# One program order over the twelve scan units of an RWKV-7 layer, the pieces of an inverse loaded through GpSimd's queue, and the backward direction's products first

## The chip, the cores and the metric

The kernel runs on one core of a Trainium2 chip. The metric is device time in microseconds (us) of one execution; lower is better. The profiled execution is one such run, taken apart by the hardware profiler. Engine names as in the profile: PE (TensorE matmul), PEld (its weight loads), DVE (VectorE), ACT (ScalarE), POOL (GpSimd), SP (SyncE, which here only issues DMAs; SPq is its queue).

## The reference

A two-layer trunk over 512 latent tokens and 256 context tokens of width 1024, all in float32. Each layer is a half-SwiGLU, a token mixer, and a half-SwiGLU. The mixer of the second layer is a bidirectional RWKV-7, and only its recurrence is touched here:

```
S_t = S_{t-1} (diag(w_t) - kk_t^T (a_t kk_t)) + v_t^T k_t ,   y_t = S_t r_t
```

There are 16 heads with a 64 by 64 state each. The forward and the backward direction each run over the context tokens first and then, from that state, over the latent tokens; the two outputs are added.

## The kernel before, in words

The recurrence is computed in chunks of 64 tokens. Within a chunk the steps are tied together by a triangular matrix N (64 by 64 for each head, chunk and direction), and the chunk's solution needs the inverse of (1 - N). The work is cut into 12 **units**, `todo` (line 1596): four groups `qd` of four heads, and for each of them g = 0 (context), 1 and 2 (the two halves of the latents). A unit has 256 tokens of each direction; d = 0 is forward, d = 1 backward. What is done for a unit, in this order:

- `prep_a` (L1239): ten loads on SP, from `hw` at L1246 to L at L1260, then decays, then the products KR and BK (DVE, L1294 and L1297), then **A**: for each direction d and head pair e, 16 matmuls (L1320), which DVE masks out of PSUM into N and, for latents, Ar (L1327, four evictions). These use two PSUM banks for each step. Then N of the backward direction is transposed on DVE (NT, L1332), and the 16 by 16 diagonal blocks of both directions are scattered to DRAM, 16 DMAs on SP (L1335).
- `prep_m` (L1340): POOL loads the blocks from DRAM (M, L1347), inverts them all at once, one block to a partition, in 28 dependent operations (L1353 and L1354), and stores them (`me`, L1357).
- `prep_d` (L1361): 16 DMAs on SP lay the inverted blocks into a tile **X** (L1366), each 16 partitions by 8 runs of 64 bytes. Two X tiles alternate.
- `prep_v`, `prep_t`, `prep_b`: loads of v (VU, four DMAs on SP, L1376), transposes of BK (bkt), and the products kT and W, copied to KW on ACT.
- `prep_c` (L1410): doubles the inverse from 16 to 32 to 64. Step 1 transposes X's blocks on DVE (L1416), step 2 is T (PE, L1428), step 3 is R (L1435), and so on to Y; four steps YK (L1477) apply Y; five steps follow with P (L1491).
- `scan` (L1506): the state G over four chunks, and y.

A `readout` of a group's result follows every third unit, through banks and queues shared with the rest.

The main loop at the end of `rwkv_scan` has one iteration for each unit i. An iteration runs the scan of unit i, `prep_b` and `prep_c` of unit i + 1, the last five steps of `prep_a` (the A steps) and `prep_t`, `prep_m` of unit i + 2, and the first fifteen steps of `prep_a` of unit i + 3. At its end come `prep_v` and `prep_d` of unit i + 2. `laid` interleaves these: each stream is given a count of steps and a stretch (from, to) of the iteration, its steps are spread evenly over the stretch, and all are emitted in order of these positions. `tc.manual_schedule` around an iteration makes PE, DVE, ACT and SP issue that iteration's instructions in the order of emission. POOL is left to the scheduler, and so is where instructions of one such region fall among those of another on the same engine. Every engine executes its own instructions in order.

So one dependency goes round from iteration to iteration: X of a unit must have landed for DVE's transposes and PE's T in `prep_c`; A evictions stand behind these on DVE and A matmuls on PE; from the last A come NT, the scatter, POOL's inversion, and X of the next unit.

Of the kernel before, what the change touches and what calls it, by code (L numbers as in the profile page):

```python
# [73 lines left out]
def trunk(ctx, tc, io, phases=None, dump=None):  # L74
# [1109 lines left out]
    def rwkv_scan(l):  # L1184
# [11 lines left out]
        def Q(name):  # L1196

            if "B2" not in late:
                name = {"N": "Ar", "NT": "L"}.get(name, name)
            name = {"bvl": "N", "gl": "N", "q": "KW"}.get(name, name)  # L1200
            ring = RINGS2.get(name) if "B2" in late else None
            return (late["B2"] if ring else B1).tile([128, 1024], F32, tag=name, name=name, bufs=ring or RINGS1[name])
# [36 lines left out]
        def prep_a(qd, g):  # L1239
# [46 lines left out]
            for d in range(2):  # L1286
# [21 lines left out]
                dve.tensor_copy(g2[:, :, 3], Ev[:, :, chunk(d, 3), end])  # L1308
                dve.tensor_copy(gs[:, 2 * d:2 * d + 2], Eiv[:, :, chunk(d, 0), beg])
                yield  # L1310
            for d in range(2):

                N[d] = Q("N").rearrange("p (s n) -> p s n", n=64)
                if lat:
                    Ar[d] = Q("Ar").rearrange("p (s n) -> p s n", n=64)
                for e in range(2):
                    ps_ = [bank("A", "a") for _ in range(2)]
                    for c in range(4):
                        for hp in range(2):
                            pe.matmul(ps_[hp][:, 128 * c:128 * c + cols], BK[d][half(hp), 4 * e + c].rearrange("p s n -> p (s n)"),  # L1320
                                      KR[d][half(hp), 4 * e + c][:, :1 + lat], start=True, stop=True)
                    for hp in range(2):
                        pv = ps_[hp].rearrange("p (c s n) -> p c s n", s=2, n=64)
                        s0 = slot(hp, e, 0)
                        for s, dst in ((0, N[d]), (1, Ar[d])):
                            if dst is not None:
                                dve.tensor_tensor(dst[:, s0:s0 + 4], pv[:, :, s],  # L1327
                                                  masks[d][:, 64 * s:64 * s + 64].unsqueeze(1).to_broadcast([128, 4, 64]), ALU.mult)
                    yield

            NT_ = Q("NT").rearrange("p (s n) -> p s n", n=64)
            dve.transpose(NT_.rearrange("p s n -> p (s n)"), N[1].rearrange("p s n -> p (s n)"))  # L1332
            md = dram.tile([128, 16, 16], F32, tag="md", name="md", bufs=2)
            for d, hp, b, l0, r0 in lanes:
                nc.sync.dma_start(out=md[l0:l0 + 8].rearrange("l s t -> s l t"),  # L1335
                                  in_=(N[0] if d == 0 else NT_)[r0:r0 + 16, 8 * hp:8 * hp + 8, 16 * b:16 * b + 16])
            ready[qd, g] = KR, BK, N, Ar, gt, md
            yield

# [21 lines left out]
        def prep_d(qd, g):  # L1361
            me = inverse[qd, g]
            X = inverse[qd, g] = diagonal[(3 * qd + g) % 2]
            for d, hp, b, l0, r0 in lanes:
                o = 16 * (b % 2)
                nc.sync.dma_start(out=X[r0:r0 + 16, d, d, :, o:o + 16], in_=me[l0:l0 + 8].rearrange("l s t -> s l t"))  # L1366
            yield

        bkts, vus = {}, {}
# [40 lines left out]
        def prep_c(qd, g):  # L1410
# [60 lines left out]
            for d in range(2):  # L1471
                for e in range(2):
                    p = bank("YK")
                    pv = p.rearrange("p (c x n) -> p c x n", c=4, x=2)
                    for c in range(4):
                        for hp in range(2):
                            pe.matmul(p[half(hp), 128 * c:128 * c + 128], Y[half(hp), d, 4 * e + c], KW[d][half(hp), e, c].rearrange("p x n -> p (x n)"), start=True, stop=True)  # L1477
                    act.activation(KW[d][:, e, :, 0], pv[:, :, 0], AF.Copy)
                    for hp in range(2):
                        if hp:  # L1480
                            dve.tensor_copy(VU[half(hp), d, :, hp, e], pv[half(hp), :, 1])
                        else:
                            act.activation(VU[half(hp), d, :, hp, e], pv[half(hp), :, 1], AF.Copy)
                    yield
            for d in range(2):
                for e in range(2):
# [19 lines left out]
        def scan(qd, g, KR, Ar, BKT, VU, gt):  # L1506
            lat = g > 0
            if g == 1:
                state["y"] = late["B2"].tile([128, 2, TL], F32, tag="y", name="ybuf", bufs=2)
            yb = state.get("y")  # L1510
            G = state["G"] if lat else None
            at = lambda d, e: slice(64 * (2 * d + e), 64 * (2 * d + e) + 64)
            if g < 2:

                dve.tensor_tensor(gt[:, :, 3], gt[:, :, 3], decays[qd, g + 1], ALU.mult)
            Gs = []
            for i in range(4):
                cs = (i, 3 - i)
                Gs.append(G)
                if g < 2 or i < 3:  # L1520
                    p = bank("G", "s")
                    for n, (d, e) in enumerate(DE):
                        for hp in range(2):
                            pe.matmul(p[half(hp), at(d, e)], BKT[d][:, e, cs[d], half(hp)], VU[:, d, cs[d], hp, e], start=n == 0, stop=True, skip_group_check=n > 0)
                    if G is not None:
                        for n, (d, e) in enumerate(DE):
                            for hp in range(2):
                                pe.matmul(p[half(hp), at(d, e)], KR[d][half(hp), 4 * e + cs[d], 0], G[half(hp), 2 * d + e], start=False, stop=True, skip_group_check=True)
                    G = late["B2"].tile([128, 4, 64], F32, tag="G", name="G", bufs=NG)
                    dve.tensor_tensor(G, p[:, :256].rearrange("p (s n) -> p s n", n=64), gt[:, :, i].unsqueeze(2).to_broadcast([128, 4, 64]), ALU.mult)  # L1530
                    yield
            state["G"] = G
            for i in (1, 3) if lat else ():

                p = bank("y", "s")
                pv = p.rearrange("p (q d e n) -> p q d e n", q=2, d=2, e=2)
                two = [(q, d, e, hp) for q in range(2) for d, e in DE for hp in range(2)]
                where = lambda q, d: (i - 1 + q, q) if d == 0 else (4 - i - 1 + 1 - q, 1 - q)
                for n, (q, d, e, hp) in enumerate(two):
                    c, o = where(q, d)  # L1540
                    pe.matmul(pv[half(hp), o, d, e], VU[:, d, c, hp, e], Ar[d][:, slot(hp, e, c)], start=n < 2, stop=True, skip_group_check=n > 1)
                for n, (q, d, e, hp) in enumerate(two):
                    c, o = where(q, d)
                    pe.matmul(pv[half(hp), o, d, e], Gs[i - 1 + q][half(hp), 2 * d + e], KR[d][half(hp), 4 * e + c, 1], start=False, stop=True, skip_group_check=True)
                for d in range(2):
                    t0 = starts(g)[d] + 64 * where(0 if d == 0 else 1, d)[0]
                    dst = yb[:, :, t0:t0 + 128].rearrange("p e (q n) -> p q e n", q=2)
                    if g == 1:
                        act.activation(dst, pv[:, :, d], AF.Copy)
                    else:  # L1550
                        dve.tensor_tensor(dst, dst, pv[:, :, d], ALU.add)
                yield
# [69 lines left out]
        run(chain(prep_d(*todo[0]), prep_v(*todo[0]), prep_t(*todo[0])))  # L1622
        run(both(chain(units[1], prep_t(*todo[1])), chain(prep_b(*todo[0]), prep_c(*todo[0]))))
        run(chain(prep_m(*todo[1]), prep_v(*todo[1]), islice(units[2], 15), prep_d(*todo[1])))
        for i, k in enumerate(todo):
            stage = lambda f, n: f(*todo[i + n]) if i + n < len(todo) else iter(())
            ahead = units[i + 3] if i + 3 < len(todo) else iter(())
            c = stage(prep_c, 1)
            y = scan(*k, *ready.pop(k))
            with tc.manual_schedule(engines=ORDERED | {mybir.EngineType.SP}):  # L1630
                laid((y, 4, 0, 0.36), (islice(ahead, 1), 1, 0.1, 0.3),
                     (stage(prep_b, 1), 2, 0, 0.3), (c, 5, 0.06, 0.44),
                     (units[i + 2] if i + 2 < len(todo) else iter(()), 5, 0.02, 0.4), 
                     (chain(stage(prep_t, 2), stage(prep_m, 2)), 4, 0.4, 0.62), (y, 2, 0.4, 0.8), (c, 4, 0.46, 0.7), (c, 5, 0.72, 0.99),
                     (islice(ahead, 14), 14, 0.5, 1.0), (out, 16, 0.0, 0.98))
                if k[1] == 2:
                    out = readout(k[0], state["y"], to_dram)
                run(chain(stage(prep_v, 2), stage(prep_d, 2)))
# [190 lines left out]
```

## Time and profile before

| | |
|---|---|
| time, median of 3 runs | 3906.98 us (3896.73 to 3912.19) |
| profiled execution: its own time, its span | 3908.28 us, 3906.5 us |
| busy share of the span | PE 91%, PEld 80%, DVE 64%, ACT 34%, POOL 28% |
| mean granted TensorE clock | 0.945 |
| DMA queues q1 (SP) and q0 (POOL), share of 16 engines | 29.6% and 0.2% |

Busy time is the time in which an engine had an instruction in work; PE's can be long only because its clock is low. The granted clock is a share of full speed: 1.0 is 2.4 GHz and 0.5 is 1.2 GHz. A wait is an engine's idle time ahead of an instruction, put down to what released it. The chain of waits is the work that ended last, followed back from the end. The twelve units take the stretch from about 2820 to 3430 us of the span.

### The profile page before, as it was taken

The page shows a single profiled execution, that of the slowest core. Times are in us where ns is not written, and L with a number is a line of the kernel's source. Part 1 is how long each engine was busy: PE and PEld are TensorE (multiplying, and loading weights), DVE is VectorE, ACT ScalarE, POOL GpSimd, SP SyncE. Part 2 cuts the span into 40 slices and gives each one's busy share as a digit, 9 for nine tenths or more (in the row PEclk, how much of TensorE's full clock was granted, in tenths as well). Part 3 has the DMA queues.
Part 4 walks back from the last instruction along what each step waited for, and adds up shares of the span by engine and source line. Part 5 has one row for each costly group of instructions (what it writes and reads, how often), then busy time and mean ns, then how long its engine had stood idle before and what let it go on. Part 6 is the DMA issues. An engine that isn't in the chain of part 4 may idle for free.

```text
span 3906.5 us, 71705 instructions
## 1 busy us (share of the span) xinstructions
PE 3545.2 (91%) x29954; PEld 3127.6 (80%) x29954; DVE 2506.8 (64%) x4108; ACT 1346.8 (34%) x2080; POOL 1093.3 (28%) x1011
## 2 busy tenths in 40 slices
PE   5999998899999799999899999698978888789998
PEld 3898997788887688888799998576867777668887
DVE  6666667656666766666766675766344444468886
ACT  4332333232322532333433333444323332244343
POOL 4212213433433422212422222522122120123332
PEclk9999999999999899999999999798988888789999
DMA  5332331411112233333132232257522222132332
GB/s 184 111 102 87 97 98 44 119 39 44 44 38 71 68 110 104 98 124 98 61 96 82 93 92 75 74 165 241 151 66 63 73 71 75 37 103 89 93 97 78
DMA packets 519395, 356.91 MB, mean 91 GB/s; under 512 B 86589, under 2 KB 493405, under 8 KB 519070
## 3 DMA queue, kind: packets, MB, share of 16 engines
q1 hardware_dynamic: 516766, 347.08, 29.6%
q8 instruction: 235, 3.85, 0.4%
q0 software_dynamic: 1152, 3.15, 0.2%
q10 hardware_dynamic: 1152, 2.10, 0.2%
q14 instruction: 90, 0.74, 0.1%
HBM read 312.52 MB, written 39.72 MB: 90 GB/s over the span
## 4 chain that ended last, share of the span: by engine, by line
PE 34%; DVE 7%; SPq 3%; DMA 3%; issue 2%; POOL 2%; ACT 1%; DVEq 0%; POOLq 0%; ACTq 0%
PE po L607 8%; PE c L534 6%; PE a L534 4%; PE b L534 3%; SPq L1366 2%; PE k L222 2%; PE v L222 1%; PE A L1320 1%; PE o L222 1%; PE bkt L295 1%; PE YK L1477 1%; DVE mx L960 1%; DVE wlo L527 1%; POOL M L1354 1%; POOL mt L1353 1%
## 5 line engine op out<-in xcount | busy, mean ns | idle before, releaser
L607 PE MATMUL po<-g,whi 128*128 128x512 f32 (+1 forms) x2464 | 592.4, 350 | 10.6 <-ACT g L211 10.2
L534 PE MATMUL c<-u,whi 128*128 128x386 f32 (+1 forms) x2112 | 522.9, 331 | 48.8 <-DVE uu L565 15.1
L526 ACT ACTIVATE whi<-raw 128x1024 fp32r<-128x1024 f32 x352 | 332.7, 950 | 568.4 <-PE po L607 308.2
L551 POOL TENSOR_TENSOR raw<-raw 128x512 f32<-128x512 f32 x88 | 125.0, 1421 | 1346.8 <-DMA raw<-in_ffn_w_in 750.9
L607 PEld LDWEIGHTS po<-g,whi 128*128 128x128 f32 x2464 | 405.6, 190 | 84.7 <-issue 11.4
L527 DVE TENSOR_TENSOR wlo<-raw,whi 128x1024 fp32r<-128x1024 f32 x352 | 411.6, 1173 | 32.3 <-ACT whi L526 30.5
L534 PEld LDWEIGHTS c<-u,whi 128*128 128x128 f32 x2112 | 370.3, 190 | 76.1 <-ACT u L446 28.3
L534 PE MATMUL a<-u,whi 128*128 128x386 f32 (+1 forms) x1408 | 349.3, 332 | 22.4 <-DVE u L428 17.2
L607 PE MATMUL po<-g,wlo 128*128 128x512 f32 (+1 forms) x1232 | 366.8, 348 | 0.0
L611 DVE SCALAR_TENSOR_TENSOR h<-po,mod,h 128x512 f32<-128x512 f32 (+1 forms) x384 | 228.2, 628 | 193.5 <-PE po L607 193.2
L534 PE MATMUL b<-u,whi 128*128 128x386 f32 (+1 forms) x1408 | 343.6, 328 | 2.8 <-DVE u L449 1.4
L534 PE MATMUL c<-u,wlo 128*128 128x386 f32 (+1 forms) x1056 | 344.3, 326 | 0.0
L196 ACT ACTIVATE whi<-raw 128x1024 fp32r<-128x1024 f32 (+1 forms) x193 | 184.6, 959 | 267.3 <-PE c L534 108.5
L534 PEld LDWEIGHTS a<-u,whi 128*128 128x128 f32 x1408 | 253.1, 193 | 28.1 <-issue 18.4
L534 PEld LDWEIGHTS b<-u,whi 128*128 128x128 f32 x1408 | 246.3, 189 | 12.8 <-issue 6.6
L534 PE MATMUL a<-u,wlo 128*128 128x386 f32 (+1 forms) x704 | 234.1, 333 | 0.5 <-DVE wlo L527 0.5
L607 PEld LDWEIGHTS po<-g,wlo 128*128 128x128 f32 x1232 | 207.7, 190 | 29.8
L534 PE MATMUL b<-u,wlo 128*128 128x386 f32 (+1 forms) x704 | 229.0, 325 | 0.4 <-DVE wlo L527 0.4
L197 POOL TENSOR_TENSOR wlo<-raw,whi 128x1024 fp32r<-128x1024 f32 x48 | 127.1, 2650 | 299.1 <-ACT whi L196 280.4
L534 PEld LDWEIGHTS c<-u,wlo 128*128 128x128 f32 x1056 | 202.8, 192 | 0.0
L197 DVE TENSOR_TENSOR wlo<-raw,whi 128x768 fp32r<-128x768 f32 (+1 forms) x145 | 171.8, 1187 | 39.3 <-ACT whi L196 39.1
L316 POOL TENSOR_TENSOR nsq<-nsq 128x768 f32<-128x768 f32 (+1 forms) x49 | 101.7, 2076 | 218.4 <-ACT nsq L314 195.5
(393 smaller groups left out, 7158.5 us busy)
## 6 DMA issues: line engine op xcount, KB each, us to landing
raw<-in_ffn_w_in SPq DMA_DIRECT2D x176, 512.0 KB
raw<-in_mod_w SPq DMA_DIRECT2D x144, 512.0 KB
raw<-in_ffn_w_out SPq DMA_DIRECT2D x80, 384.0 KB
raw<-in_hgrn_w_in SPq DMA_DIRECT2D x40, 512.0 KB
raw<-in_ffn_w_out SPq DMA_DIRECT2D x28, 512.0 KB
raw<-in_w_rkv SPq DMA_DIRECT2D x24, 512.0 KB
L<-s_bk SPq DMA_DIRECT2D x48, 256.0 KB
s_bk<-knb SPq DMA_DIRECT2D x32, 192.0 KB
```

The lines of the kernel that those rows point to most:

```text
L196: act.activation(hi[:, :m], raw[:, :m], AF.Copy)
L197: slots["lo"].tensor_tensor(lo[:, :m], raw[:, :m], hi[:, :m].bitcast(F32), ALU.subtract)
L222: pe.matmul(p[:, q:q + t1 - t0], a[:, k, c0:c0 + 128], b[:, t0:t1], start=(k == 0 and i == 0), stop=(k == nk - 1 and i == 2))
L295: pe.matmul(p, x, ident, start=True, stop=True)
L316: pool.tensor_tensor(sq[:, :n], acc[:, :n], sq[:, :n], ALU.add)
L526: act.activation(hi, x, AF.Copy)
L527: dve.tensor_tensor(lo, x, hi.bitcast(F32), ALU.subtract)
L534: pe.matmul(p[:, :q], a[:, c], x[k][:, b], start=first and k == 0 and i == 0, stop=k == 3 and i == 2, skip_group_check=not first)
L551: pool.tensor_tensor(S[:, lo], U[:, lo], U[:, hi], ALU.add)
L607: pe.matmul(p[v][:, :t1 - t0], wx[:, k, at:at + 128], x[:, e, t0:t1], start=k == 0 and i == 0, stop=k == nk - 1 and i == 2)
L611: dve.scalar_tensor_tensor(h[d][:, t0:t1], p[v][:, :t1 - t0], mods[l, sub, 2][:, d, v:v + 1], h[d][:, t0:t1], ALU.mult, ALU.add)
L1366: nc.sync.dma_start(out=X[r0:r0 + 16, d, d, :, o:o + 16], in_=me[l0:l0 + 8].rearrange("l s t -> s l t"))
```

## The change

The diff does five things. One `manual_schedule` region is put around the whole loop in place of one for each iteration. X's sixteen pieces are issued from POOL's queue instead of SP's. In `prep_a` the A steps run d = 1 first, and each direction's scatter follows its own A steps. In `laid`, the A steps move from the stretch 0.02 to 0.4 to the stretch 0 to 0.3, the first five `prep_c` steps from 0.06 to 0.44 to 0.14 to 0.5, and `prep_b` ends earlier; for context units, all four A steps now fall in that stretch (two were in the iteration before). In the YK steps, DVE instead of ACT copies the first half (128 by 256), and ACT copies both parts of the second half (64 by 256 each), of which DVE had one.

```
-            for d in range(2):
+            md = dram.tile([128, 16, 16], F32, tag="md", name="md", bufs=2)
+
+            def scatter(d, x):
+                for d_, hp, b, l0, r0 in lanes:
+                    if d_ == d:
+                        nc.sync.dma_start(out=md[l0:l0 + 8].rearrange("l s t -> s l t"), in_=x[r0:r0 + 16, 8 * hp:8 * hp + 8, 16 * b:16 * b + 16])
+
+            for d in (1, 0):
...
-            NT_ = Q("NT").rearrange("p (s n) -> p s n", n=64)
-            dve.transpose(NT_.rearrange("p s n -> p (s n)"), N[1].rearrange("p s n -> p (s n)"))
-            md = dram.tile([128, 16, 16], F32, tag="md", name="md", bufs=2)
-            for d, hp, b, l0, r0 in lanes:
-                nc.sync.dma_start(out=md[l0:l0 + 8].rearrange("l s t -> s l t"),
-                                  in_=(N[0] if d == 0 else NT_)[r0:r0 + 16, 8 * hp:8 * hp + 8, 16 * b:16 * b + 16])
+                if d:
+                    NT_ = Q("NT").rearrange("p (s n) -> p s n", n=64)
+                    dve.transpose(NT_.rearrange("p s n -> p (s n)"), N[1].rearrange("p s n -> p (s n)"))
+                    scatter(1, NT_)
+                else:
+                    scatter(0, N[0])
...
-                nc.sync.dma_start(out=X[r0:r0 + 16, d, d, :, o:o + 16], in_=me[l0:l0 + 8].rearrange("l s t -> s l t"))
+                pool.dma_start(out=X[r0:r0 + 16, d, d, :, o:o + 16], in_=me[l0:l0 + 8].rearrange("l s t -> s l t"))
...
-                    act.activation(KW[d][:, e, :, 0], pv[:, :, 0], AF.Copy)
+                    dve.tensor_copy(KW[d][:, e, :, 0], pv[:, :, 0])
                     for hp in range(2):
-                        if hp:
-                            dve.tensor_copy(VU[half(hp), d, :, hp, e], pv[half(hp), :, 1])
-                        else:
-                            act.activation(VU[half(hp), d, :, hp, e], pv[half(hp), :, 1], AF.Copy)
+                        act.activation(VU[half(hp), d, :, hp, e], pv[half(hp), :, 1], AF.Copy)
...
-        for i, k in enumerate(todo):
...
-            with tc.manual_schedule(engines=ORDERED | {mybir.EngineType.SP}):
+        with tc.manual_schedule(engines=ORDERED | {mybir.EngineType.SP}):
+            for i, k in enumerate(todo):
...
+                after = 14 if i % 3 else 12
...
                 laid((y, 4, 0, 0.36), (islice(ahead, 1), 1, 0.1, 0.3),
-                     (stage(prep_b, 1), 2, 0, 0.3), (c, 5, 0.06, 0.44),
-                     (units[i + 2] if i + 2 < len(todo) else iter(()), 5, 0.02, 0.4), 
-                     (chain(stage(prep_t, 2), stage(prep_m, 2)), 4, 0.4, 0.62), (y, 2, 0.4, 0.8), (c, 4, 0.46, 0.7), (c, 5, 0.72, 0.99),
-                     (islice(ahead, 14), 14, 0.5, 1.0), (out, 16, 0.0, 0.98))
+                     (stage(prep_b, 1), 2, 0, 0.24), (c, 5, 0.14, 0.5),
+                     (units[i + 2] if i + 2 < len(todo) else iter(()), 5, 0, 0.3),
+                     (chain(stage(prep_t, 2), stage(prep_m, 2)), 4, 0.4, 0.62), (y, 2, 0.4, 0.8), (c, 4, 0.5, 0.73), (c, 5, 0.74, 0.99),
+                     (islice(ahead, after), after, 0.5, 1.0), (out, 16, 0.0, 0.98))
```

## Rows read from the trace of the kernel before

**Rows 1.** The page's chain that ended last, its shares by line.
```profile
PE po L607 8%; PE c L534 6%; PE a L534 4%; PE b L534 3%; SPq L1366 2%; PE k L222 2%; PE v L222 1%; PE A L1320 1%; PE o L222 1%; PE bkt L295 1%; PE YK L1477 1%; DVE mx L960 1%; DVE wlo L527 1%; POOL M L1354 1%; POOL mt L1353 1%
```

**Rows 2.** POOL's timeline, stores of `me`: start us, us, engine, line, operation.
```profile
2859.21 0.58 POOL L1357 DMA_DIRECT2D me<-M  x1 [0.30 <-POOL M L1354]
...
3222.45 0.58 POOL L1357 DMA_DIRECT2D me<-M  x1 [0.30 <-POOL M L1354]
...
3383.14 0.58 POOL L1357 DMA_DIRECT2D me<-M  x1 [0.30 <-POOL M L1354]
```

**Rows 3.** Busy time by stretch: length, PE, PEld, DVE, ACT, POOL, clock, DMA.
```profile
2868.00:3391.00 523.00, 438.18 (x10024) 380.17 (x10024) 235.85 (x622) 156.33 (x350) 95.72 (x310) 0.83 0.25 64
3143.50:3157.00 13.50, 12.33 (x323) 11.08 (x324) 6.98 (x15) 6.28 (x13) 0.54 (x1) 1.00 0.15 33
3157.00:3179.00 22.00, 18.48 (x286) 14.90 (x280) 11.61 (x31) 7.73 (x20) 10.43 (x30) 0.92 0.15 37
3186.00:3196.00 10.00, 9.30 (x220) 8.59 (x223) 4.72 (x19) 1.71 (x3) 0.00 (x0) 0.50 0.46 128
```

**Rows 4.** The chain of waits through one period: start us, us, what.
```profile
3132.84 0.45 DVE X L1416
...
3147.65 1.17 DVE NT L1332
...
3152.05 3.21 DMA md<-NT
...
3159.18 0.21 POOL mt L1353
...
3160.07 0.07 issue
...
3171.38 2.02 DMA me<-M
...
3182.80 1.61 DMA X<-me
```

**Rows 5.** SP's timeline: loads of X, and around one scatter.
```profile
2861.25 7.43 SPq L1366 DMA_DIRECT2D X<-me  x16
...
3129.85 0.38 SPq L1257 DMA_DIRECT2D KR<-s_kk  x1
...
3134.65 5.83 SPq L1335 DMA_DIRECT2D md<-N  x8
...
3237.14 9.00 SPq L1366 DMA_DIRECT2D X<-me  x16
...
3391.76 9.11 SPq L1366 DMA_DIRECT2D X<-me  x16
```

**Rows 6.** Groups by line, 2868 to 3391: busy, mean ns, idle before.
```profile
L1428 PE MATMUL T<-X,N 32*32 32x32 f32 x1280 | 21.0, 212 | 13.0 <-DMA X<-me 11.2 <-DVE X L1416 1.8
L1435 PE MATMUL R<-X,t 32*32 32x32 f32 x1280 | 15.8, 207 | 11.5 <-ACT KW L1408 7.4 <-issue 4.2
L1327 DVE TENSOR_TENSOR N<-A,cst 128x256 f32<-128x256 f32 x78 | 31.1, 410 | 21.7 <-PE A L1320 21.6
```

**Rows 7.** Waits of DVE, 2868 to 3391: total us, times, longest.
```profile
DVE VU L1481 <- ACT VU L1483: 101.5, 40, 5.2
DVE X L1416 <- DMA X<-me: 51.9, 16, 4.6
```

**Rows 8.** Line 1357: duration of POOL's store in ns, min/median/max.
```profile
L1357 POOL DMA_DIRECT2D me<-M x12: 585/585/587, 2786.2 to 3383.1; - x12
```

**Rows 9.** POOL's timeline: one operation of L1353 (128x26) in two periods.
```profile
3102.78 0.23 POOL L1353 TENSOR_TENSOR mt<-M 128x26 f32<-128x26 f32 x1
...
3169.06 0.78 POOL L1353 TENSOR_TENSOR mt<-M 128x26 f32<-128x26 f32 x1
```

**Rows 10.** DVE's timeline: BK of the backward direction.
```profile
3124.50 1.28 DVE L1297 TENSOR_TENSOR BK<-L,Ei 128x512 f32<-128x512 f32 x2
```

**Rows 11.** PE's timeline: the iteration's first A step, forward.
```profile
3124.56 1.16 PE L1320 MATMUL A<-KS,BK 64*128 64x128 f32 x16
```

More of the change, by code (lines that the diff above doesn't have):

```diff
@@ L1624, in rwkv_scan @@
         run(chain(prep_m(*todo[1]), prep_v(*todo[1]), islice(units[2], 15), prep_d(*todo[1])))
-        for i, k in enumerate(todo):
[L1626 to L1629, printed above, removed]
-            with tc.manual_schedule(engines=ORDERED | {mybir.EngineType.SP}):
+        with tc.manual_schedule(engines=ORDERED | {mybir.EngineType.SP}):
+            for i, k in enumerate(todo):
+                stage = lambda f, n: f(*todo[i + n]) if i + n < len(todo) else iter(())
+                ahead = units[i + 3] if i + 3 < len(todo) else iter(())
+                after = 14 if i % 3 else 12
+                c = stage(prep_c, 1)
+                y = scan(*k, *ready.pop(k))
                 laid((y, 4, 0, 0.36), (islice(ahead, 1), 1, 0.1, 0.3),
-                     (stage(prep_b, 1), 2, 0, 0.3), (c, 5, 0.06, 0.44),
-                     (units[i + 2] if i + 2 < len(todo) else iter(()), 5, 0.02, 0.4),
-                     (chain(stage(prep_t, 2), stage(prep_m, 2)), 4, 0.4, 0.62), (y, 2, 0.4, 0.8), (c, 4, 0.46, 0.7), (c, 5, 0.72, 0.99),
-                     (islice(ahead, 14), 14, 0.5, 1.0), (out, 16, 0.0, 0.98))
+                     (stage(prep_b, 1), 2, 0, 0.24), (c, 5, 0.14, 0.5),
+                     (units[i + 2] if i + 2 < len(todo) else iter(()), 5, 0, 0.3),
+                     (chain(stage(prep_t, 2), stage(prep_m, 2)), 4, 0.4, 0.62), (y, 2, 0.4, 0.8), (c, 4, 0.5, 0.73), (c, 5, 0.74, 0.99),
+                     (islice(ahead, after), after, 0.5, 1.0), (out, 16, 0.0, 0.98))
                 if k[1] == 2:
```

## The prediction, made before the changed kernel was run

> **What bounds the kernel now.** The page comes first: PE is busy for 91% of the span and the chain that ended last is PE's feed-forward matmuls, but it holds 2% for the issue of X's pieces by SP and lines of POOL's inversion [rows 1]. These are from the twelve scan units, the only stretch that the change touches. POOL's timeline gives the pace there: from the first `me` store in the stretch to the last are ten periods in 523.9 us, 52.4 us each [rows 2]. The view by stretches shows what PE does meanwhile: busy for 438 of 523 us at a mean granted clock of 0.83 [rows 3], so in one period it is busy for 43.9 us and idle for 8.5 us, and its work at full clock would be 43.9 x 0.83 = 36.4 us. The reader is to see two losses, the idle time and the low clock. The chain of waits through one period says where they come from: it leaves PE and goes round through X, the last A step, NT, the scatter, POOL and X again [rows 4]. From DVE's second transpose of X to the next X landed are 3184.4 - 3132.8 = 51.6 us, nearly the period. Its legs: 14.8 from X to NT, 1.2 NT, 3.2 eight issues of the scatter, 7.1 until POOL has the blocks, 12.2 inversion, 2.0 store, 9.4 SP's issue of X's sixteen pieces, 1.6 the last landing. PE and DVE both stand at X: T waits 13.0 us in all, R behind it 11.5, DVE 51.9 [rows 6, 7]. Behind such a wait the clock was 0.50 for 10 us (1.2 GHz), while stretches without it have 1.00 and 0.92 [rows 3].
>
> SP adds a hold. X must be issued after everything ahead of it in SP's order, such as VU's loads, which wait for scan output. For eleven X loads the time from the store's landing (2.0 us after its start) to SP's first piece is 53 us in sum: nothing at the first (2861.25), 12.7 at the longest (3237.14 against 3222.45), 6.6 at the last [rows 2, 5]. That is 5.3 us a period on average, where it is on the ring.
>
> **The change, part by part.** *A in the first third, backward direction first.* In the new order three of the four A steps come ahead of DVE's transposes of X (positions 0.03, 0.09, 0.15 against 0.176), NT has gone by, and PE's T (0.248) is behind all four. Behind X the ring then has one transpose and the four evictions of the last A, 0.45 + 4 x 0.41 = 2.1 us [rows 4, 6], in place of 14.8 + 1.2. So 13.9 us leave the ring.
>
> *X's pieces on POOL.* The trace has no piece on POOL. The nearest row is POOL's store of 128 KB, also 128 runs, 0.585 us in all twelve cases [rows 8]; with 0.07 us between POOL's instructions [rows 4], sixteen take 10.5 us against SP's 9.4. From below nothing is excluded under 0.585, from above POOL's own operations rise from 0.23 to 0.78 us (3.4 times) in another period [rows 9], which would make a piece 1.99 and sixteen 33.0 us. I take 10.5, since twelve equal rows of a DMA stand nearer than an arithmetic operation. POOL has nothing behind the pieces but the next unit's load of M, which cannot start before the next scatter. The hold on SP goes.
>
> The trace shows that a POOL DMA kept its 0.585 us while a POOL tensor operation did not keep its 0.23 [rows 8, 9]. The Trainium skill, SBUF — State Buffer, section "SBUF: two separate sides", speaks against this edit: a DMA issued from GpSimd has its descriptors written by GpSimd, and a DVE operation in a two-port mode locks it out, so that a DMA of about 620 ns took about 3100 ns. By that, sixteen pieces would take 50.7 us and the kernel some 265 us more (an estimate from that page). No row here shows it for a DMA.
>
> *The ring after.* 2.1 + 3.2 + 7.1 + 12.2 + 2.0 + 10.5 + 1.6 = 38.7 us. It is shorter than PE's part, so PE's order sets the period.
>
> *SP's order.* The scatter of the forward blocks is now behind the backward scatter and behind unit i + 3's loads (position 0.2), eight of which take 3134.65 - 3129.85 = 4.8 us [rows 5]. With a period near 47 us: second A step at 4.2, its matmuls 1.2 [rows 11], evictions 1.6, NT 1.2, scatter 3.2, loads 4.8 give 16.2 us. X lands 36.6 us later, 52.8, which is 5.9 us into the next iteration; DVE wants it at 0.176 x 47 = 8.3 and PE at 11.7. So I cost this at nothing; the cover is 2.4 us on DVE and 5.8 on PE, and beyond it the wait for X is back.
>
> *One order over all units.* SP, PE, DVE and ACT lose the freedom to take the next iteration's first instructions early. The first A step is now the backward one, whose BK is the last product that DVE makes in an iteration: it ended at 3125.8, and the forward A step that stood there had begun at 3124.6 [rows 10, 11]. So PE waits 1.2 us more at each border; the bounds are 0 and the 5 us that three such DVE products and evictions may queue up.
>
> *The copies in YK.* DVE stood 101.5 us behind ACT's copy of the same bank, 2.5 us each of 40 times [rows 7]. It will not, but ACT then stands behind DVE, and PE's groups show no wait on these lines. DVE is busy for 45% of the stretch [rows 3]. Nothing, with 0 to 1 us a period gained as bounds. The first two X loads and A steps, ahead of the loop, I also put at nothing, give or take 5 us in all.
>
> **The sum.** PE's work stays at 36.4 us at full clock. Without the stretches at half clock I take 0.93, between the 0.92 and 1.00 that undisturbed stretches have and nearer the longer of them: 39.1 us. Idle: 8.5, less T's wait (13.0 / 10 = 1.3) and half of R's (0.6, since `prep_b`, whose copy on ACT it waited for, now comes ahead of T), plus 1.2 at the border: 7.8. Together 46.9 us a period, 5.5 less than 52.4; ten periods give 55 us. From the profiled execution's 3908.3 that is 3853; the median of the runs is 1.3 lower, so the forecast is **3852 us**. Its own range has the clock at 0.97 with 6.6 us idle (44.1, a gain of 83) and at 0.88 with 8.7 idle (50.1, a gain of 23): 3824 to 3884.
>
> **Rivals.**
> *More than that:* the copies and the ended waits also remove idle time that I left in; the period falls between the ring's 38.7 and 44.1, the time to 3777 to 3824, say 3805. For it speaks DVE's 101.5 us; against it that PE's other idle groups have nothing to do with X.
> *X late again:* the forward scatter waits for the loads and for readout's transfers on SP, beyond the 5.8 us of cover; T waits as before and the clock falls to 0.50 for 10 us, 5 us lost. Period 51, time 3893. For it speaks that SP's hold reached 12.7 us in this order; against it that the holds were at VU's loads, which now hold up nothing that X needs.
> *The order gives it back:* at each border PE stands 3 to 5 us for DVE's last products, and this idle time, not X's, brings the half clock: 46.9 + 5 = 52, no change, 3903. Or the scheduler had already given this order, and the regions change nothing.
> *Slower, POOL's pieces:* place: POOL's queue between the store and X. Without the pieces the ring is 28.2 us; it decides the period from 46.9 on, that is from 1.17 us a piece, and is as slow as before at 1.51 (52.4 - 28.2 over 16). At the 2.06 of the upper bound the period is 61.2 and the time 3907 + 88 = 3995. For it: rows 9. Against: rows 8. The rule of the Trainium skill above is this mechanism, with its own price.
>
> **How the numbers follow.** Forecast 0.47, more than that 0.13, X late again 0.14, order gives it back 0.11, POOL's pieces 0.15. A measurement of this kernel tells a difference from none at about 0.5%, 20 us: 3887 to 3927. Faster is the forecast, the case above it and a third of X late again: 0.65. The same: the rest of that case, the border case and a little of POOL's: 0.21. Slower: 0.14. The range 3800 to 3915 holds the forecast, most of the better case, X late again and nearly all of the border case, 0.8 in all.
>
> **What would show it.** Right: `me` stores some 47 us apart; DVE's wait for X under 1 us a unit; T's wait near nothing; POOL issuing sixteen pieces in 10 to 11 us right after the store; a granted clock of 0.9 or more over the stretch; a wait of about 1 us of the first A step for BK. Wrong: pieces of 1.2 us or more on POOL; T still waiting for X; PE idle for over 3 us at each border; or a stretch as long as before with no wait on X in it.

## The result, and the profile after

| | before | after |
|---|---|---|
| median of the runs | 3901.86 us (4) | 3861.47 us (4) |
| ratio of the runs, 95% interval | | 0.9896, 0.9875 to 0.9917 |
| profiled execution | 3908.28 us | 3863.86 us |

The change is 1.0% faster: 40.4 us by the medians, 44.4 us by the two profiled executions. The forecast was 3852 us, 55 us of gain; its range 3800 to 3915.

The pace of the twelve units first, by POOL's timeline of the changed kernel, which answers to [rows 2, 5]: stores `me` and the pieces of X behind them.

```profile
2857.96 0.60 POOL L1364 DMA_DIRECT2D me<-M  x1 [0.30 <-POOL M L1361]
2860.55 8.37 POOL L1373 DMA_DIRECT2D X<-me  x16 [1.99 <-issue]
...
3142.05 0.60 POOL L1364 DMA_DIRECT2D me<-M  x1 [0.30 <-POOL M L1361]
3144.67 8.37 POOL L1373 DMA_DIRECT2D X<-me  x16 [2.02 <-DVE BK L1297]
...
3191.47 8.37 POOL L1373 DMA_DIRECT2D X<-me  x16 [2.01 <-DVE KW L1485]
...
3337.51 0.60 POOL L1364 DMA_DIRECT2D me<-M  x1 [0.30 <-POOL M L1361]
```

Ten periods take 479.6 us, 48.0 each, where they took 52.4. That is 44.4 us, as much as the two profiled executions differ by (ahead of these periods 1.3 us are gained, behind them 1.2 lost). The sixteen pieces begin about 2 us behind the store, 4.2 at the last, and take 8.4 us. The stretch itself, with the columns of [rows 3]:

```profile
2868.00:3345.00 477.00, 392.19 (x9792) 344.56 (x9792) 226.27 (x608) 156.12 (x347) 168.42 (x462) 0.88 0.29 74
```

It holds 9.95 periods: in each PE is busy for 39.4 us (43.9 before) and idle for 8.5 (8.5 before), at a clock of 0.88 (0.83). Cut exactly from store to store, the ten periods have 434.6 us of busy time before and 396.7 after: 37.9 of the 44.4 us are busy time that became shorter, and 6.5 are idle time. PE does the same matmuls at a higher clock: in the clock's records it stands at half (1.2 GHz) for 181 us of the ten periods before, and for 116 us after. The idle time is nearly as long as it was, but it lies elsewhere. PE's waits in this stretch (total us, times, longest), to set beside [rows 6]:

```profile
PE A L1327 <- DVE BK L1297: 23.0, 9, 3.2
PE R L1442 <- issue: 16.2, 10, 3.5
PE TT L1460 <- DVE AT L1445: 11.9, 8, 1.6
PE P L1495 <- ACT VU L1487: 8.4, 13, 1.8
PE TT L1460 <- issue: 6.9, 4, 2.1
```

T's wait for X is gone; the first A step's wait for BK has come, and idle time at R and TT, the next steps of the same chain. Two large waits of the kernel before (2868 to 3391) are no longer among PE's:

```profile
PE kT L1404 <- DVE KR L1496: 9.8, 1, 9.8
PE bkt L295 <- ACT Y L1465: 9.6, 7, 2.9
```

DVE's waits, against [rows 7]:

```profile
DVE KW L1485 <- PE YK L1484: 33.4, 13, 3.9
...
DVE X L1423 <- DMA X<-me: 2.0, 1, 2.0
```

One period of the chain of waits, for [rows 4, 10, 11] (start, us, what):

```profile
3148.38 0.61 DVE BK L1297
3149.03 1.16 PE A L1327 x16
...
3157.23 0.73 DVE NT L1340
...
3163.16 1.56 PE T L1435 x96
3164.72 1.61 issue
...
3168.06 1.32 PE R L1442 x86
3169.38 1.52 issue
3170.90 0.86 PE R L1442 x42
3171.78 0.70 DVE A L1444
...
3201.21 1.61 PE A L1327 x16
```

The backward A step begins when DVE's last BK ends. No leg of this period belongs to SP, to POOL's inversion or to X's landing, which made up most of [rows 4].

The legs called issue, idle time in which PE waited for nothing that the profile shows, need a second look. The one at 3169.38 lies inside a step: 86 of R's 128 matmuls run, PE stands for 1.52 us, and the other 42 run. So do all of R's, TT's and T's issue waits in this stretch: they are pauses within a step and not handoffs between steps, such as TT's 11.9 us for AT. With the other lines, PE's issue waits come to 31.6 us in the stretch, and to 17.4 in the 523 us of the kernel before. The trace has something that goes with them, transfers of 16 KB on a queue that is called instruction (packets, MB, share):

```profile
q8 instruction: 236, 3.87, 0.4%
```

In the stretch they number 77, about one for every 256 of PE's matmuls and weight loads, and each of PE's 22 pauses of over 0.3 us ends 2.3 to 2.9 us after one of them began. An engine that waits for its own instructions would look like this; no run here tests it.

### The profile page after: what moved, and what is told of

The parts are those of the page before. It is cut to its first block, busy times and chain, and to the rows that moved or that the text cites. A ratio compares the mean times of both kernels' runs of the same rounds, so it can differ in the third digit from the quotient of the medians.

```text
span 3862.1 us, 71805 instructions
## 1 busy us (share of the span) xinstructions
PE 3500.5 (91%) x29954; PEld 3093.4 (80%) x29954; DVE 2505.7 (65%) x4108; ACT 1349.6 (35%) x2080; POOL 1190.1 (31%) x1203
## 3 DMA queue, kind: packets, MB, share of 16 engines
q10 hardware_dynamic: 1152, 2.10, 0.2%
```

## The experiments

All were timed beside the kernel before. "Changed" is the changed kernel. Ratios are to the kernel before; a difference of 0.2% (8 us) between two of these is about what their intervals can hold.

| run | median us | ratio, 95% interval | period us |
|---|---|---|---|
| changed, again | 3852.9 | 0.9878, 0.9857 to 0.9899 | 48.0 |
| X on SP | 3858.7 | 0.9894, 0.9873 to 0.9915 | 47.5 |
| A late | 3896.6 | 0.9997, 0.9983 to 1.0012 | 52.2 |
| products backward first | 3840.2 | 0.9851, 0.9829 to 0.9872 | 46.2 |
| X on POOL alone | 3905.3 | 1.0008, 0.9996 to 1.0021 | 51.9 |
| region for each iteration | 3860.5 | 0.9888, 0.9872 to 0.9905 | 47.1 |
| YK copies back | 3869.8 | 0.9910, 0.9896 to 0.9925 | 48.6 |
| twice the pieces | 3863.3 | 0.9899, 0.9884 to 0.9914 | 48.4 |
| A early alone | 3867.2 | 0.9915, 0.9899 to 0.9932 | 48.6 |
| forward first | 3840.9 | 0.9846, 0.9830 to 0.9862 | 45.6 |
| scan between | 3836.0 | 0.9832, 0.9815 to 0.9850 | 45.6 |
| scan and bkt between | 3840.4 | 0.9851, 0.9833 to 0.9870 | 46.2 |

**The yardstick.** 

> The changed kernel itself again, as the yardstick for the runs beside it. Both theories (the gain comes from moving A ahead of X; the gain comes from taking X off SP's order): a ratio of 0.990 to the kernel before, some 40 us.

The ratio came out at 0.9878; the two measurements of the changed kernel, 0.9896 and 0.9878, are 0.2% apart and their intervals overlap.

**X on SP.**
```
-                pool.dma_start(out=X[...], in_=me[...])
+                nc.sync.dma_start(out=X[...], in_=me[...])
```


> The changed kernel with X's sixteen pieces back on SP's queue. Theory 1, moving A ahead of X is what gains: in the changed kernel's trace POOL's store has landed about 14 us before SP has its next backward scatter to issue (3144.0 against 3158.4 us), so SP's 9 us of X fit in between and the period stays at 48 to 49.5 us, 0 to 15 us slower than the changed kernel. Rival, the queue is what gains: SP's hold of 5 us a period is back, with a stretch at half clock behind it, and 30 to 50 us of the gain are gone, so that the time is about that of the kernel before.

Theory 1 holds: the time is within the yardstick's, and the period of 47.5 us is even below its 48 to 49.5. SP's timeline shows X between the loads of v and the next backward scatter, as expected:

```profile
3131.54 2.58 SPq L1383 DMA_DIRECT2D VU<-s_v  x4
3143.45 8.52 SPq L1373 DMA_DIRECT2D X<-me  x16
...
3157.01 3.89 SPq L1316 DMA_DIRECT2D md<-NT  x8
```

**A late.** The old order of A steps, the old scatter and the old positions (`prep_a` and `laid` as before), the rest as changed.
```
-            for d in (1, 0):
+            for d in range(2):
...
-                     (units[i + 2] if i + 2 < len(todo) else iter(()), 5, 0, 0.3),
+                     (units[i + 2] if i + 2 < len(todo) else iter(()), 5, 0.02, 0.4),
```


> The changed kernel with the A steps, their order of directions, the scatter and all positions of the interleaving as before; one region, X on POOL and the YK copies stay as changed. Theory 1: the ring has its 16 us of A steps and NT again and is 34.5 + 16.0 = 50.5 us with POOL's 8.4 us of pieces; the period is 50.5 to 52 us and 25 to 40 us of the gain are gone. DVE's wait for X is back at over 3 us a unit. Rival (the queue): most of the gain stays, within 10 us of the changed kernel.

All of the gain is gone, 35 to 44 us against the changed kernel's two measurements where Theory 1 had 25 to 40; the period of 52.2 us is just above its interval. X is waited for again, on PE and on DVE:

```profile
PE T L1428 <- DVE X L1416: 15.6, 3, 6.4
PE bkt L295 <- ACT Y L1465: 8.0, 6, 2.9
PE T L1428 <- DMA X<-me: 7.9, 8, 2.1
```

```profile
DVE X L1416 <- DMA X<-me: 39.5, 8, 7.6
```

So X on POOL, the one order and the YK copies together give nothing while the A steps stand behind X.

**X on POOL alone**, on the kernel before (the edit of X on SP, reversed).

> The kernel before with one edit alone, X's pieces from POOL's queue. Theory 1 (A ahead of X is what gains, the queue alone does not): the ring is still 51.6 less about 1 us for the faster issue (8.4 for 9.4), so where a unit was not held by SP nothing is gained; the holds of 5.3 us a period lay partly beside PE's own work. 0 to 15 us faster than the kernel before. Rival (the queue gains): 30 to 50 us faster.

No gain: 1.0008, at the lower end of what Theory 1 allowed. DVE still waits for X:

```profile
DVE X L1416 <- DMA X<-me: 39.4, 10, 6.4
```

Ending SP's holds, 5.3 us a period, gave nothing back.

**A early alone**, on the kernel before: the two hunks that "A late" takes out, and nothing else.

> The kernel before with one edit alone: the A steps backward first with their own scatters, and the new positions of the interleaving. X stays on SP, one region for each iteration, YK copies as before. Theory 1 (this edit is the gain, the other three are worth up to 10 us together): period 48 to 50 us, 25 to 40 us faster than the kernel before. Rival (the gain needs the edits together, since the hold on SP comes back without POOL's queue and the one order): 0 to 15 us faster.

33 us faster, in Theory 1's interval: this edit is most of the change. It is a bundle itself (A earlier, the scatter split by direction, `prep_b` ended earlier, X's own steps later), and no run takes its parts one by one. DVE's wait for X fell to

```profile
DVE X L1423 <- DMA X<-me: 3.3, 2, 2.2
```

with X on SP. What the other three edits add lies between this run and the two of the changed kernel, 6 to 14 us by the medians, with intervals that touch.

**A region for each iteration.**
```
-        with tc.manual_schedule(engines=ORDERED | {mybir.EngineType.SP}):
-            for i, k in enumerate(todo):
+        for i, k in enumerate(todo):
...
+            with tc.manual_schedule(engines=ORDERED | {mybir.EngineType.SP}):
```


> The changed kernel with one region for each iteration, as before, and all other edits kept. Theory 1: the one order as such is worth nothing or costs a little at the border; PE's wait for BK (23 us in ten periods) shrinks where the scheduler takes other PE work early, and the time is 0 to 10 us below the changed kernel's. Rival: without the one order, instructions of the next iteration's X wait come ahead of the A steps again on some engine, and 10 to 30 us of the gain are lost.

The time is the changed kernel's (0.9888), as Theory 1 allowed, but its reason did not come: the border's wait is unchanged to a tenth of a us:

```profile
PE A L1327 <- DVE BK L1297: 23.0, 9, 3.2
```

The one order is worth nothing that can be measured in the time, and it is not what makes PE wait at the border. The period by POOL's stores is 47.1 us, 8 us less in ten, without a shorter time: differences of that size between the periods of the table prove nothing by themselves.

**YK copies back.**
```
-                    dve.tensor_copy(KW[d][:, e, :, 0], pv[:, :, 0])
+                    act.activation(KW[d][:, e, :, 0], pv[:, :, 0], AF.Copy)
```
(and the second half shared between DVE and ACT again.) 

> The changed kernel with the copies of the YK steps as before (ACT, ACT, DVE). DVE's wait of 2.5 us a step behind ACT is back, 100 us in all. Theory 1, which put these copies at nothing, with 0 to 1 us a period as bounds: 0 to 10 us slower than the changed kernel. Rival: DVE's blocked time was the real gain, since DVE's last products now set the border; PE's wait for BK doubles and the time is 20 us or more above the changed kernel's.

8 to 17 us by the medians over the changed kernel's two measurements, intervals touching. The rival's sign is absent: PE's wait for BK stayed at 22.4 us. DVE's blocked time came back by half of what was expected:

```profile
DVE VU L1488 <- ACT VU L1490: 47.3, 36, 3.5
```

Whether these copies are worth nothing or some 17 us stays open.

**Twice the pieces.**
```
-                pool.dma_start(out=X[r0:r0 + 16, d, d, :, o:o + 16], in_=me[l0:l0 + 8].rearrange("l s t -> s l t"))
+                for q in (0, 4):
+                    pool.dma_start(out=X[r0:r0 + 16, d, d, q:q + 4, o:o + 16], in_=me[l0 + q:l0 + q + 4].rearrange("l s t -> s l t"))
```


> The changed kernel with each of X's sixteen pieces cut in two, so that POOL issues 32 a unit. At 0.52 us each, X lands 8 us later. Theory 1 (the ring of some 37 us is well inside the period of 48): PE reaches T about 7 us after X has landed, so the delay is nearly all covered, 0 to 20 us slower, with DVE's wait for X back at 2 to 4 us a unit. Rival: X still sets the period, and each us on POOL is a us a period, 60 to 85 us slower.

POOL took 16 us a unit instead of 8.4, and the wait for X is back in the profile on both engines, yet the period is 48.4 for 48.0 and the ratio the same:

```profile
PE R L1443 <- issue: 9.9, 8, 2.8
...
PE T L1436 <- DMA X<-me: 7.8, 8, 2.5
```

```profile
DVE X L1424 <- DMA X<-me: 33.3, 8, 7.0
```

PE now stands 7.8 us at T, and R's pauses are 6.3 us shorter than the changed kernel's 16.2. A wait that is not on a ring may be lengthened for nothing: 8 us of added delay a unit cost 0.5 us a period, if anything.

**Products backward first**, and **forward first**: two ways to end the border's wait.
```
-            for d in range(2):
+            for d in (1, 0):
                 E, Ei = EEs[d]
```


> The changed kernel with DVE's products KR and BK also made for the backward direction first, so that the first A step of an iteration finds its BK ready. Theory: PE's wait of the A steps for BK, 23.0 us in the ten periods, falls under 8 us, and the time by 10 to 20 us. Rival: the wait is only passed on, since the border has too little work for PE and the forward BK or other DVE work is then late; the time stays within 5 us.

```
-            for d in (1, 0):
+            for d in range(2):

                 N[d] = Q("N").rearrange("p (s n) -> p s n", n=64)
```


> The changed kernel with the forward direction's A steps first, at the same early positions, each direction's scatter behind its own steps. PE's wait for the backward BK at the border is gone (23 us in ten periods), and NT (1.2 us) and the backward scatter are last before X. Theory 1 (the positions ahead of X gain, the order of directions does not; X has some 7 us of cover): 5 to 20 us faster than the changed kernel, like the kernel that made the products backward first. Rival (the backward direction first is needed, since NT at the end puts X late again): 10 us or more slower than the changed kernel.

Both are faster, 12 to 21 us by the medians against the changed kernel's two measurements; the second's interval (to 0.9862) lies below that of the first measurement (from 0.9875) and just touches the second's (from 0.9857). BK is no longer among PE's waits in either. In the second X stays covered though NT now comes last (DVE waits 3.4 us for X in all):

```profile
PE R L1442 <- issue: 23.1, 11, 4.0
PE TT L1460 <- DVE AT L1445: 13.5, 9, 1.6
PE P L1495 <- ACT VU L1487: 8.6, 13, 2.0
PE W L1413 <- DMA VU<-s_v: 4.8, 4, 2.8
```

```profile
2868.00:3345.00 477.00, 401.50 (x10537) 352.80 (x10538) 235.44 (x630) 162.50 (x359) 176.02 (x477) 0.91 0.30 77
```

The clock rose to 0.91. So the early positions gain, and the order of directions that came with them took back a fifth to a third of it (12 to 21 of 60 us).

**Scan between**, and **scan and bkt between**, on top of products backward first.
```
-                laid((y, 4, 0, 0.36), ...
+                laid((y, 4, 0, 0.4), ...
```


> Products backward first (the kernel 12 us below the changed one) and the four steps of the scan spread over 0 to 0.4 of an iteration instead of 0 to 0.36, so that one of them stands between T and R and one between R and TT. PE's waits ahead of R (12.8 us) and TT (20 us in ten periods) fall together by 10 us or more; 5 to 12 us faster than with the products alone. Rival: the scan's state G is a chain of its own, later steps make y and the next iteration late, and nothing is gained.

```
-                     (chain(stage(prep_t, 2), stage(prep_m, 2)), 4, 0.4, 0.62), ...
+                     (chain(stage(prep_t, 2), stage(prep_m, 2)), 4, 0.33, 0.62), ...
```


> As the run with the scan between, and the transposes bkt start at 0.33 instead of 0.4, so that one stands between R and TT and one between TT and the step after it. PE's wait ahead of TT falls under 8 us in ten periods; another 5 to 10 us faster. Rival: bkt's copies on ACT stand behind the four copies of Y (2.5 us), hold the two shared PSUM banks, and cost what they fill; no faster or up to 10 us slower.

The first is 4 us below products backward first, less than the 5 to 12 expected and inside the intervals; as a version it is the fastest run here, 1.7% below the kernel before and clear of the changed kernel. TT's wait, in products backward first

```profile
PE TT L1460 <- DVE AT L1445: 12.5, 9, 1.6
PE TT L1460 <- issue: 7.6, 4, 2.7
```

fell, with other PE work laid into the handoff from R to TT (the part behind AT from 12.5 to 0.6 us); R's, 12.8 us there, did not:

```profile
PE R L1442 <- issue: 13.7, 9, 2.8
...
PE TT L1460 <- issue: 2.7, 2, 1.5
```

The second kept TT's wait as low, but R's rose, and nothing was gained:

```profile
PE R L1442 <- issue: 24.0, 11, 3.1
```

That is the rival's outcome, though its reason (the two shared banks) was not shown: these 24.0 us are again pauses inside the step. Neither edit, laying work between steps, made them shorter.

## Why the prediction was right, point by point

**The ring, and A ahead of X.** Right, and the heart of it. The ring was taken to set the period at 51.6 us. With A late the period is 52.2; with A early it is 48, and there the ring no longer sets it, since 8 us more on POOL cost 0.5. From the iteration's first A step to X landed 52.8 us were forecast; in the period above the last piece ends at 3199.84, and with the 1.6 us of [rows 4] for its landing that is 52.4 after 3149.03 (49 to 56 over ten units). The bundle was credited as one, though: the positions carry the gain, and "backward direction first" costs 12 to 21 us, shown by forward first.

**X on POOL.** The size was nearly right (10.5 us forecast, 8.4 measured) and so was its place beside the path, but 5.3 us a period of SP's hold (53 us over eleven loads, so 4.9 a load) were listed as a loss without a sum that used them. The runs give them nothing: X on POOL alone 1.0008, X on SP 0.9894. The rule of the Trainium skill (SBUF — State Buffer, "SBUF: two separate sides") that DVE in a two-port mode can hold up GpSimd's descriptors did not bear here: the 192 pieces took, in ns, min/median/max,

```profile
L1373 POOL DMA_DIRECT2D X<-me x192: 528/528/553, 2799.2 to 3350.2; - x192
```

with DVE busy for 226 of 477 us; from issue to landing they took 2.0 us at the median and 4.5 at the longest. Whether any of DVE's instructions was in such a mode, no run shows. The "slower" rival falls by the same row.

**One order; copies; SP's order.** All put at nothing. The order measured nothing (a region for each iteration), the copies 0 to 17 us, SP's loads ahead of the forward scatter cost nothing because X had cover left (twice the pieces).

**The border.** The mechanism was right, BK as the last product that DVE makes, and the term was mis-sized: 1.2 us a period forecast, 2.3 measured (23.0 in ten). It stood under the one order, but the run without the one order has the same 23.0; the two runs that end the wait show that it comes of taking the backward A step first while its products are made last. [Rows 10, 11] are one border of the kernel before; the changed kernel's nine waits run from 1.9 to 3.2 us. Why they are longer than that one border is open.

**The sum.** Period 46.9 forecast, 48.0 measured; ten of them are the 11 us between the forecast gain and the profiled one. Idle 7.8 forecast, 8.5 measured. T's 13.0 us for X and R's 7.4 behind `prep_b`'s copy did go, as forecast. The step that failed as stated is "half of R's": R's idle time grew from 1.15 to 1.6 us a period, and TT's, which the sum did not have, from 0.2 to 1.9. Of TT's, 1.2 is the handoff from R over DVE with too little other PE work laid between, which scan between shows; the rest of it and all of R's are the pauses inside a step, whose cause stays open. That the total is near is partly luck: kT's and bkt's waits, 1.9 us a period in the kernel before, went too, and the forecast had left them in. The clock came to 0.88, not 0.93, and missed the 0.9 named as a sign of being right: the stretches at half clock became shorter and did not go. That the busy time agreed all the same, 39.1 forecast and 39.4 measured, is luck: PE's full-clock work, worked out as busy time by mean clock, is only a rough product (36.4 before, 34.7 after, for the same matmuls), and the two errors cancel. The other rivals fall too: the period stayed above 44.1, T's wait for X is gone, and the border's 2.3 us are below the 3 to 5 that would have given the gain back.

## What to carry to other kernels

Look for the dependency that comes back to the same engine one iteration later, add its legs, and compare the sum with the period: only work taken off that ring shortens it, and in a fixed order it can be taken off by placing its producer ahead of the wait in each queue. Once the ring is shorter than the busiest engine's part, neither the queue of the transfer nor doubling its length mattered here, though its wait was long in the profile. When a step moves to the front of an iteration, look up which of its inputs is made last: here, making that input first gave back 12 to 21 us. And before laying work into an idle stretch, look where it lies: a pause inside a step is no handoff, and work laid between steps did not shorten it here.

## What the runs showed of the hardware that was not expected

The same 192 small DMAs (128 runs of 64 bytes each) made far fewer packets from POOL's queue than from SP's. From before to after the queue of SP fell from 516766 packets, and POOL's rose from 1152, to

```profile
q1 hardware_dynamic: 489118, 345.49, 29.9%
q0 software_dynamic: 7296, 4.73, 0.8%
```

that is 144 packets a DMA on SP's and 32 on POOL's. POOL issued them about as fast, 0.53 us each and 8.4 for sixteen, as SP, whose sixteen took 7.4 to 9.8 us in the stretch before. In one of the twelve loads POOL stood still for 2.4 us after its third piece; why is open.

PE's pauses inside a step, 31.6 us in the 477 of the stretch, each 2.3 to 2.9 us after a 16 KB transfer on the instruction queue began, were not expected either.
